# A mixture-of-experts kernel's end: the loop for surplus tokens moved behind the last up products, and the last down weights, down products and final norm done by column halves

## The chip, the cores and the metric

The kernel runs on one core of a Trainium2 chip. The metric is the device time of one execution in microseconds (us); lower is better. Engines are named as in the profile: PE is TensorE (PEld its weight loads), DVE is VectorE, ACT is ScalarE, POOL is GpSimd, and SP is the engine whose queue issues nearly all DMAs here. A letter q behind a name (SPq, PEq) means the engine's sequencer.

## The reference, cut to what matters

One layer over 256 tokens of width 1024: a norm, a projection, an mLSTM half and a differential-attention half, an output projection, then a hierarchical mixture of 32 experts and a last norm. Only the end of it is touched by the change:

```
    t = h.reshape(-1, d)                       # h = rmsnorm(x, norm2_g)
    ...                                        # router: 2 experts of one group per token, gates
    for e in range(N_EXPERTS):                 # 32 experts, width 512
        hid = jax.nn.silu(t @ w_eg[e]) * (t @ w_eu[e])
        out = out + gates[:, e:e + 1] * (hid @ w_ed[e])
    x = x + out
    return rmsnorm(x, normf_g)
```

Each of `w_eg`, `w_eu` and `w_ed` is 2 MB per expert in float32, so the expert weights alone are 192 MB.

## The kernel before

The kernel computes each expert only on the tokens that chose it. 128 slots (partitions) are shared by a group of two experts with 64 slots each or of four experts with 32 slots each; the last group has four. For each group PE gathers its tokens, transposed, with a one-hot matrix (`prep`), multiplies them by the gate and up weights (`gate`, `up`, L885), takes silu times up times the gate value, transposes that (`hidden`, L820 on DVE, L824 on PE, L827 on ACT), multiplies by the down weights (`down`, L902), splits the result into a high and a low part (ACT, then DVE) and scatters both back by a one-hot matrix into four PSUM accumulators `acc[j][t]`, where j is the half of the 1024 output columns and t the half of the 256 tokens. With four experts of 32 slots, a matmul uses 32 of PE's columns, and four matmuls of four experts run side by side; such a set of four is called a quad here.

Weights come in tiles of 1 MB: one expert, one half `hf` of the rows of a weight matrix (for `w_ed`: hf 0 holds the row blocks k = 0 and 1, hf 1 holds k = 2 and 3, each 1024 columns wide). SP issues these DMAs in the order gate, up, down of each group (`load`, `load_w`). Eight counters ("lanes") count landed DMAs in turn; each issue waits until the DMA eight places before it has landed, so that at most eight are open. In the last group (`LAST`), the tiles of hf 1 of `w_ed` come in three pieces: k = 2 whole (512 KB), then the two column halves of k = 3 (256 KB each).

An expert can have more tokens than slots. The surplus is done by a loop whose count `n_ov` is worked out on the chip (L1018 to L1077). Every engine reads `n_ov`, and branches. Where it is 0, an engine jumps to a block that adds to the counters what its own part of the loop would have added; SP's block also waits for the lanes that the loop's DMAs would use. So the loop stands in all engines' instruction streams even when no pass runs, and in the profiled execution none runs.

In the program, the loop stands right behind the last gate product. Behind the loop come the last `up` (`pu_l`, L1080), `hidden` into the tile `hT_l` (L1083), the final norm's gains spread over the partitions (`nfb`, L1087 on PE and L1088 on ACT), the last down products (L1094), their split (L1100, L1101), the scatter (L1105), and the final norm: `square` (L1109, sums of squares on ACT), `gain` (L1113, times `nfb` on DVE), `rms` (L1116 and L161 to L167) and `scale` with the output DMA (L1122 to L1127). `keep_warm` (L186) issues matmuls whose result nobody reads; their numbers between the last down products are `NW5`. Within an engine, instructions run in the order of the built program; a scheduler may move rows within a block, but none over the loop.

Of the kernel before, what the change touches and what calls it, by code (L numbers as in the profile page):

```python
# [10 lines left out]
F32 = mybir.dt.float32  # L11
# [5 lines left out]
OP = mybir.AluOpType  # L17
AX = mybir.AxisListType

P = 128  # L20
S = 256
NT = 2
D = 1024
KD = 8
H = 4
NE = 32
# [3 lines left out]
FF = 512  # L30
# [7 lines left out]
NWA, NWB, NWZ = 6, 11, 6  # L38
NPJ = 4
NST = 4  # L40
NWARM, NW1, NW2, NW3, NW5 = 9, 2, 10, 4, (0, 8, 4, 0)
NL = 3


# [1 line left out]
R_CW, R_CB, R_MN, R_MS, R_DA, R_N1, R_N2, R_NF = 0, 16, 20, 24, 28, 29, 37, 45  # L46
# [58 lines left out]
def kernel(ctx: ExitStack, tc: tile.TileContext,  # L105
                       x, w_in, w_out, w_eg, w_eu, w_ed, pack_a, pack_b, pack_m, out, dbg=None):
    nc = tc.nc
    V, A, G, T, SY = nc.vector, nc.scalar, nc.gpsimd, nc.tensor, nc.sync
    PS = bass.MemoryType.PSUM

    def dap(t, off, ap):
        return bass.AP(tensor=t.tensor, offset=t.offset + off, ap=ap)
# [26 lines left out]
    ident = ca[:, A_ID:A_ID + P]  # L139
# [3 lines left out]
    def col(i):  # L143
        return ca[:, A_COL + i:A_COL + i + 1]
# [10 lines left out]
    behind = [None, None]  # L155
# [25 lines left out]
    def keep_warm(n, pw, after=None):  # L181

        wide = warm[:, None, :].to_broadcast([P, 4, P])
        for _ in range(n):
            if after is None:
                T.matmul(pw, warm, wide, start=True, stop=True)  # L186
            else:
                with tc.issue_after(after.ins):
                    after = T.matmul(pw, warm, wide, start=True, stop=True)
# [92 lines left out]
    o = proj_T(0)  # L282
# [44 lines left out]
    o = proj_tok(512)  # L327
# [67 lines left out]
    o = proj_T(1536)  # L395
# [3 lines left out]
    o = proj_T(2048)  # L399
# [15 lines left out]
    o = proj_tok(2560)  # L415
    wo = []
    for j in range(2):
        for kk in (1, 0):
            w = w_half()
# [18 lines left out]
    for h in range(H):  # L438
# [115 lines left out]
    o = proj_T(1024, {2: po_ends[0], 4: po_ends[1], 5: po_ends[2], 6: po_ends[3]})  # L554
# [17 lines left out]
    acc = [[pacc.tile([P, 512], F32, name=f"acc{j}{t}") for t in range(NT)] for j in range(2)]  # L572
# [28 lines left out]
    for b, (c0, nc_) in enumerate(cols):  # L601
        j, cj = c0 // 512, c0 % 512
# [12 lines left out]
        for i in range(c0 // 256, (c0 + nc_) // 256):  # L615
# [16 lines left out]
            for m in range(2):  # L632
# [3 lines left out]
                for t in range(NT):  # L636
                    c = (m - first) * S + t * P
# [38 lines left out]
    def top8(name, v):  # L676
# [4 lines left out]
        for t in range(NT):  # L681
# [9 lines left out]
                    op=OP.not_equal)  # L691
# [47 lines left out]
    def pmm():  # L739
        return psm.tile([P, 512], F32, name="pmm", tag="pmm", bufs=4)  # L740
# [5 lines left out]
    order = [wa] + wbs[:7] + [wa] + wbs[7:9] + [wa] + wbs[9:] + [wa] + wzs[:2] + [wa] * 2 + wzs[2:]  # L746
    count, loaded = [0], [None]
# [6 lines left out]
    LAST = len(groups) - 1  # L754
    assert sum(map(len, groups)) == NE and len(groups[LAST]) == 4

    def load_w(src, rows, hf, pieces):

        w = []
        for _ in rows:  # L760
            w.append(order[count[0] % len(order)].tile([P, 4, 512], F32, name="w", tag="w"))
            count[0] += 1
        w = [v.rearrange("p a b -> p (a b)") for v in w]
        at = (0, *pieces)
        for c0, c1 in zip(at, pieces):
            for i, v in enumerate(w):
                o = hf * 2048 + c0
                if isinstance(rows[i], int):
                    r = dap(src, rows[i] * D * FF + o, [[4096, P], [1, c1 - c0]])
                else:  # L770
                    if isinstance(rows[i], bass.AP):
                        rows[i] = SY.value_load(rows[i], min_val=0, max_val=NE - 1)
                    r = of_expert(src, rows[i])[:, o:o + c1 - c0]
                with tc.issue_after(loaded[0].ins) if len(pieces) > 1 else nullcontext():
                    loaded[0] = SY.dma_start(v[:, c0:c1], r)
        return w

    def of_expert(src, e):

        return src.rearrange("o e d f -> (o e) (d f)")[bass.ds(e, 1)].rearrange("e (p n) -> (e p) n", p=P)  # L780
# [31 lines left out]
    def free(i):  # L812

        w = order[(count[0] + i) % len(order)].tile([P, 4, 512], F32, name="w", tag="w")
        return w.rearrange("p a b -> p (a b)")

    def hidden(n, sg_, pu_, gs, to=None):
        hid = mp.tile([P, 512], F32R, name="oH", tag="oH", bufs=1).bitcast(F32).rearrange("p (k s) -> p k s", k=4)

        V.scalar_tensor_tensor(hid[:n], sg_[:n].rearrange("p (q k) -> p k q", k=4), gs[:n, :1],  # L820
                               pu_[:n].rearrange("p (q k) -> p k q", k=4), op0=OP.mult, op1=OP.mult)
        pt = pmm()
        for k in range(4):
            T.transpose(pt[:, k * P:k * P + n], hid[:n, k], ident[:n, :n])  # L824
        hT = mp.tile([P, 512], F32R, name="oL", tag="oL", bufs=1).bitcast(F32) if to is None else to
        hT = hT.rearrange("p (k s) -> p k s", k=4)
        A.copy(hT[:, :, :n], pt.rearrange("p (k s) -> p k s", k=4)[:, :, :n])  # L827
        return hT
# [33 lines left out]
    def load(g):  # L862
        ws = {}
        src = {"g": w_eg, "u": w_eu, "d": w_ed}
        js = groups[g]
        rows = list(js) if js[0] < N_FIX else [permi[0:1, j:j + 1] for j in js]
        for n_, hf in [(n_, hf) for hf in range(2) for n_ in "gu"] + [("d", 0), ("d", 1)] if g == 0 else \
                [(n_, hf) for n_ in "gud" for hf in range(2)]:

            at = (1024, 1536, 2048) if g == LAST and (n_, hf) == ("d", 1) else (2048,)  # L870
            for i, w in enumerate(load_w(src[n_], rows, hf, at)):
                ws[n_, i, hf] = w
        return ws

    up_end = [None]

    def up(ws, n_, xg, p_=None, ks=range(KD)):
        if p_ is None:
            p_ = pgu()
        n = len(ws) // 6  # L880
        cap = P // n
        for k in ks:
            for i in range(n):
                k4 = k % 4
                up_end[0] = T.matmul(p_[i * cap:(i + 1) * cap], xg[:, k, i * cap:(i + 1) * cap],  # L885
                         ws[n_, i, k // 4][:, k4 * FF:(k4 + 1) * FF], start=(k == 0), stop=(k == KD - 1))
        return p_
# [4 lines left out]
        A.activation(sg_, up(ws, "g", xg) if p_ is None else p_, AF.Silu, scale=rs[:, :1])  # L892
        return sg_

    def down(ws, hT, ojs, ks=range(4)):
        n = len(ws) // 6
        cap = P // n
        for k in ks:
            for j in range(2):
                for i in range(n):  # L900
                    c0 = (k % 2) * D + j * 512
                    T.matmul(ojs[j][i * cap:(i + 1) * cap], hT[:, k, i * cap:(i + 1) * cap],  # L902
                             ws["d", i, k // 2][:, c0:c0 + 512], start=(k == 0), stop=(k == 3))
        return ojs

# [73 lines left out]
    ws = load(0)  # L979
# [20 lines left out]
    for pr in range(LAST):  # L1000
# [4 lines left out]
        hT = hidden(P, sg_, pu_, gs)  # L1005
# [7 lines left out]
    room = free(0)  # L1013
    sg_l = gate(ws, xg_l, rs_l, room[:, :FF])
    wx_free = [free(i) for i in range(1, 7)]
    tc.keep_in_program_order(A.preload_act_table_set(SET_EXP_LN))

    n_ov = nc.values_load(nov[0:1, 0:1], min_val=0, max_val=2 * S // (CAP // 2 + 1))  # L1018
# [58 lines left out]
                scatter(CAP, S_, oj, j)  # L1077


    pu_l = up(ws, "u", xg_l)  # L1080

    nfb, zt, jk, hT_l = (free(i) for i in range(7, 11))
    hT_l = hidden(P, sg_l, pu_l, gs_l, hT_l[:, :512])  # L1083
    for j in range(2):
        p_ = pmm()
        for k in range(4):
            T.matmul(p_[:, k * P:(k + 1) * P], col(R_NF + 4 * j + k).to_broadcast([P, P]), ident, start=True, stop=True)  # L1087
        A.copy(nfb[:, j * 512:(j + 1) * 512], p_)  # L1088
    ss = mp.tile([P, NT, 2], F32, name="ss")
    zt = [zt[:, t * D:(t + 1) * D] for t in range(NT)]  # L1090
    oj = [pgu(), pgu()]
    warm_to = pgu()
    for k, n in enumerate(NW5):
        down(ws, hT_l, oj, (k,))  # L1094
        if n:
            keep_warm(n, warm_to)
    oH = [jk[:, j * 512:(j + 1) * 512].bitcast(F32R) for j in range(2)]
    oL = [jk[:, (2 + j) * 512:(3 + j) * 512].bitcast(F32R) for j in range(2)]
    for j in range(2):
        A.copy(oH[j], oj[j])  # L1100
        V.tensor_tensor(oL[j], oj[j], oH[j].bitcast(F32), op=OP.subtract)  # L1101
    for o_ in (oH, oL):
        for j in range(2):
            for t in range(NT):
                T.matmul(acc[j][t], S_l[:, t * P:(t + 1) * P], o_[j], start=False, stop=(o_ is oL), skip_group_check=True)  # L1105

    def square(j, t):
        sq = mp.tile([P, KD, P], F32, name="xg", tag="xg", bufs=1).rearrange("p k s -> p (k s)")[:, :FF]
        A.activation(sq, acc[j][t], AF.Square, accum_out=ss[:, t, j:j + 1])  # L1109

    def gain(j, t):
        js = slice(j * 512, (j + 1) * 512)
        V.tensor_tensor(zt[t][:, js], acc[j][t], nfb[:, js], op=OP.mult)  # L1113
# [12 lines left out]
            V.tensor_scalar(z, z, rf, None, op0=OP.mult)  # L1126
        (A if E is A else SY).dma_start(dap(out, t * P * D + i * 512, [[D, P], [1, 512]]), z)  # L1127

    square(0, 0)
    gain(0, 0)  # L1130
    gain(0, 1)
    square(1, 0)
    rf = rms(0)
    square(0, 1)
    with tc.issue_after(behind[1].ins):
        gain(1, 0)
    with tc.issue_after(behind[0].ins):
        square(1, 1)
    scale(0, 0, V, rf)
    scale(0, 1, V, rf)  # L1140
    rf = rms(1)
# [30 lines left out]
```

## Time and profile before

| | |
|---|---|
| median of 3 runs | 613.75 us (613.34 to 614.83) |
| the profiled execution's own time | 614.0 us |
| its span, first to last instruction | 612.2 us |
| mean granted PE clock | 0.953 of full |
| PE busy | 537.4 us (88%) |
| DVE, ACT, POOL busy | 163.5, 124.5, 8.9 us |
| read from HBM | 221.39 MB, 365 GB/s over the span |

Outside the span lie 614.0 - 612.2 = 1.8 us. The page's table of 40 slices shows DMA at nine tenths or more from slice 15 to slice 38 at about 420 GB/s, and 37 and 69 GB/s in the last two slices. Its PE row reads 9 in nearly all of the middle, and 3, 8 and 3 in the last three slices. Most of the span is thus a stream of weights; the change touches what stands at the end of that stream.

### The profile page before, as it was taken

The page shows a single profiled execution, that of the slowest core. Times are in us where ns is not written, and L with a number is a line of the kernel's source. Part 1 is how long each engine was busy: PE and PEld are TensorE (multiplying, and loading weights), DVE is VectorE, ACT ScalarE, POOL GpSimd, SP SyncE. Part 2 cuts the span into 40 slices and gives each one's busy share as a digit, 9 for nine tenths or more (in the row PEclk, how much of TensorE's full clock was granted, in tenths as well). Part 3 has the DMA queues.
Part 4 walks back from the last instruction along what each step waited for, and adds up shares of the span by engine and source line. Part 5 has one row for each costly group of instructions (what it writes and reads, how often), then busy time and mean ns, then how long its engine had stood idle before and what let it go on. Part 6 is the DMA issues. An engine that isn't in the chain of part 4 may idle for free. (4 is left out here: it accounts for less than half of the span.)

```text
span 612.2 us, 8083 instructions
## 1 busy us (share of the span) xinstructions
PE 537.4 (88%) x3047; PEld 271.5 (44%) x3047; DVE 163.5 (27%) x472; ACT 124.5 (20%) x291; POOL 8.9 (1%) x19
## 2 busy tenths in 40 slices
PE   7999999998999999999799788799787799786383
PEld 5898779794543424344325223225223225221120
DVE  4774788745230202020200100100100100100004
ACT  4775477662100000010000000000100000010013
POOL 0000004001000000000000000000000000000000
PEclk8999999999999999999899799899989899798877
DMA  8965798968999999999999999999999999999911
GB/s 297 390 185 118 241 401 347 391 247 331 337 373 425 386 421 420 420 420 418 420 419 420 419 420 419 422 419 418 420 421 419 419 420 418 421 419 419 396 37 69
DMA packets 40764, 223.77 MB, mean 366 GB/s; under 512 B 3732, under 2 KB 6164, under 8 KB 16532
## 3 DMA queue, kind: packets, MB, share of 16 engines
q1 hardware_dynamic: 40436, 222.89, 91.0%
q8 instruction: 25, 0.41, 0.3%
q10 hardware_dynamic: 288, 0.35, 0.3%
q14 instruction: 15, 0.12, 0.0%
HBM read 221.39 MB, written 1.84 MB: 365 GB/s over the span
## 5 line engine op out<-in xcount | busy, mean ns | idle before, releaser
L885 PE MATMUL pmm<-w,xg 128*32 128x512 f32 (+1 forms) x1024 | 203.5, 624 | 18.3 <-DMA w<-in_w_eu_dram 13.5
L885 PEld LDWEIGHTS pmm<-w,xg 128*32 128x32 f32 (+1 forms) x1024 | 52.0, 123 | 140.1 <-issue 97.4
L902 PE MATMUL pmm<-w,oL 128*32 128x512 f32 (+1 forms) x448 | 97.6, 653 | 10.4 <-ACT oL L827 6.1
L902 PEld LDWEIGHTS pmm<-w,oL 128*32 128x32 f32 (+1 forms) x448 | 29.6, 131 | 70.9 <-issue 46.2
L233 DVE TENSOR_TENSOR wl<-w,wh 128x512 fp32r<-128x512 f32 (+1 forms) x72 | 44.6, 630 | 24.3 <-ACT wh L232 22.2
L834 DVE TENSOR_TENSOR oL<-pmm,oH 128x512 fp32r<-128x512 f32 x20 | 13.8, 691 | 133.5 <-PE pmm L902 104.3
L232 ACT ACTIVATE wh<-w 128x512 fp32r<-128x512 f32 (+1 forms) x72 | 41.0, 581 | 29.8 <-PE pj L263 13.1
L807 PEld LDWEIGHTS pmm<-Gm,x1c 128*128 128x128 f32 x352 | 40.6, 192 | 14.3 <-PE pmm L885 7.4
L807 PE MATMUL pmm<-Gm,x1c 128*128 128x128 f32 x352 | 43.8, 280 | 0.6 <-DVE ctr L977 0.6
L263 PE MATMUL pj<-hL,wh 128*128 128x256 f32 x128 | 36.3, 289 | 0.0
L833 ACT CAST oH<-pmm 128x512 fp32r<-128x512 f32 x20 | 11.7, 585 | 120.4 <-PE pmm L902 95.2
L261 PE MATMUL pj<-hH,wh 128*128 128x256 f32 x128 | 35.8, 291 | 0.0
L264 PE MATMUL pj<-hH,wl 128*128 128x256 f32 x128 | 35.7, 290 | 0.0
L808 DVE TENSOR_TENSOR xg<-pmm,cb 128x512 f32<-128x512 f32 (+1 forms) x24 | 14.9, 644 | 75.5 <-PE pmm L885 63.7
L827 ACT COPY oL<-pmm 128x512 f32<-128x512 f32 x10 | 5.8, 585 | 137.5 <-PE pmm L824 137.5
L892 ACT ACTIVATE oL<-pmm,rg 128x512 f32<-128x512 f32 x10 | 6.9, 687 | 89.3 <-PE pmm L885 64.9
L263 PEld LDWEIGHTS pj<-hL,wh 128*128 128x128 f32 x128 | 24.6, 192 | 0.1
L264 PEld LDWEIGHTS pj<-hH,wl 128*128 128x128 f32 x128 | 24.1, 192 | 1.4 <-issue 1.2
L261 PEld LDWEIGHTS pj<-hH,wh 128*128 128x128 f32 x128 | 24.3, 193 | 0.2
L902 PE MATMUL pmm<-w 128*32 128x512 f32 x64 | 11.9, 684 | 11.1 <-ACT w L827 11.1
L824 PE MATMUL pmm<-ca,oH 128*128 128x128 f32 x44 | 7.1, 283 | 16.2 <-DVE oH L820 16.2
L820 DVE SCALAR_TENSOR_TENSOR oH<-oL,rg,pmm 128x512 f32<-128x512 f32 x10 | 11.2, 1119 | 25.8 <-PE pmm L885 22.7
(344 smaller groups left out, 481.9 us busy)
## 6 DMA issues: line engine op xcount, KB each, us to landing
w<-in_w_eg_dram SPq DMA_DIRECT2D x64, 1024.0 KB, 19.8
w<-in_w_eu_dram SPq DMA_DIRECT2D x64, 1024.0 KB, 19.8
w<-in_w_ed_dram SPq DMA_DIRECT2D x60, 1024.0 KB, 19.8
w<-in_w_in_dram SPq DMA_DIRECT2D x10, 1024.0 KB, 14.4
w<-in_w_out_dram SPq DMA_DIRECT2D x4, 1024.0 KB, 12.8
w<-in_w_ed_dram SPq DMA_DIRECT2D x4, 512.0 KB, 17.8
w<-in_w_ed_dram SPq DMA_DIRECT2D x8, 256.0 KB, 7.8
w<-in_w_in_dram SPq DMA_DIRECT2D x3, 512.0 KB, 8.7
```

The costliest lines, as they stand in the source:

```text
L232: A.activation(wh, raw, AF.Copy)
L233: V.tensor_tensor(wl, raw, wh.bitcast(F32), op=OP.subtract)
L261: T.matmul(om, wh[:, cs], hH[:, k], start=(k == 0 and m % 2 == 0), stop=False, skip_group_check=True)
L263: T.matmul(om, wh[:, cs], hL[:, k], start=False, stop=False, skip_group_check=True)
L264: T.matmul(om, wl[:, cs], hH[:, k], start=False, stop=(k == KD - 1), skip_group_check=True)
L807: T.matmul(px_[:, i * P:i * P + n], x1c[:, t, k0 + i], G_[:, t], start=(t == 0), stop=(t == NT - 1))
L808: V.tensor_tensor(xg[:, k0:k0 + per, :n], px_.rearrange("p (k s) -> p k s", k=4)[:, :per, :n], cb[:, B_N2 + k0:B_N2 + k0 + per, None].to_b ...
L820: V.scalar_tensor_tensor(hid[:n], sg_[:n].rearrange("p (q k) -> p k q", k=4), gs[:n, :1], pu_[:n].rearrange("p (q k) -> p k q", k=4), op0= ...
L833: A.copy(oH[:n], oj[:n])
L834: V.tensor_tensor(oL[:n], oj[:n], oH[:n].bitcast(F32), op=OP.subtract)
L885: up_end[0] = T.matmul(p_[i * cap:(i + 1) * cap], xg[:, k, i * cap:(i + 1) * cap], ws[n_, i, k // 4][:, k4 * FF:(k4 + 1) * FF], start=(k = ...
L902: T.matmul(ojs[j][i * cap:(i + 1) * cap], hT[:, k, i * cap:(i + 1) * cap], ws["d", i, k // 2][:, c0:c0 + 512], start=(k == 0), stop=(k == 3))
```

## The change

1. The last `up`, `hidden` and the two `nfb` products and copies stand ahead of the loop; ACT's table load, the reading of `n_ov`, and the loop follow them.
2. `load_w` loses its pieces. The last group's down weights are loaded by `load_by_columns`: first the left 512 columns of hf 0 and of hf 1 of all four experts (512 KB each), then the right 512 columns of hf 0 (512 KB each), of k = 2 and of k = 3 (256 KB each). That is 20 DMAs in place of 16, in runs of 2 KB per partition (512 float32 numbers).
3. The last down products, split and scatter are done for the left columns (j = 0) first and then for the right columns (`last_down`). The squares and gains of the left columns follow the left scatter; at the end ACT makes the two squares of the right columns one after the other.
4. `NW5` goes from (0, 8, 4, 0) to (8, 4, 4, 3): 8 warm matmuls between the two row halves of the left columns, 4 behind the left scatter, 4 behind k = 0 and 1 of the right columns, 3 behind k = 2.

```diff
-NWARM, NW1, NW2, NW3, NW5 = 9, 2, 10, 4, (0, 8, 4, 0)
+NWARM, NW1, NW2, NW3, NW5 = 9, 2, 10, 4, (8, 4, 4, 3)
...
+    def load_by_columns(src, rows):
+
+        w = [[slot() for _ in rows] for _ in range(2)]
+        for hf, k0, k1, j in ((0, 0, 2, 0), (1, 0, 2, 0), (0, 0, 2, 1), (1, 0, 1, 1), (1, 1, 2, 1)):
+            for v, e in zip(w[hf], rows):
+                at = [a.rearrange("p (k c) -> p k c", k=2)[:, k0:k1, j * 512:(j + 1) * 512]
+                      for a in (v, of_expert(src, e)[:, hf * 2048:(hf + 1) * 2048])]
+                with tc.issue_after(loaded[0].ins):
+                    loaded[0] = SY.dma_start(*at)
...
-            at = (1024, 1536, 2048) if g == LAST and (n_, hf) == ("d", 1) else (2048,)
-            for i, w in enumerate(load_w(src[n_], rows, hf, at)):
-                ws[n_, i, hf] = w
+            if g < LAST or n_ != "d":
+                for i, w in enumerate(load_w(src[n_], rows, hf)):
+                    ws[n_, i, hf] = w
+        if g == LAST:
+            for hf, w_ in enumerate(load_by_columns(w_ed, rows)):
+                for i, w in enumerate(w_):
+                    ws["d", i, hf] = w
...
     wx_free = [free(i) for i in range(1, 7)]
+    pu_l = up(ws, "u", xg_l)
+
+    nfb, zt, jk, hT_l = (free(i) for i in range(7, 11))
+    hT_l = hidden(P, sg_l, pu_l, gs_l, hT_l[:, :512])
+    for j in range(2):
+        p_ = pmm()
+        for k in range(4):
+            T.matmul(p_[:, k * P:(k + 1) * P], col(R_NF + 4 * j + k).to_broadcast([P, P]), ident, start=True, stop=True)
+        A.copy(nfb[:, j * 512:(j + 1) * 512], p_)
     tc.keep_in_program_order(A.preload_act_table_set(SET_EXP_LN))
 
     n_ov = nc.values_load(nov[0:1, 0:1], min_val=0, max_val=2 * S // (CAP // 2 + 1))
...
-    pu_l = up(ws, "u", xg_l)
...
-    for k, n in enumerate(NW5):
-        down(ws, hT_l, oj, (k,))
-        if n:
-            keep_warm(n, warm_to)
...
+    def last_down(j, pieces):
+        end = None
+        for ks, n in pieces:
+            with tc.issue_after((end or last_end[0]).ins):
+                down(ws, hT_l, oj, ks, (j,))
+                end = down_end[0]
+            if n:
+                keep_warm(n, warm_to, end)
+        A.copy(oH[j], oj[j])
+        V.tensor_tensor(oL[j], oj[j], oH[j].bitcast(F32), op=OP.subtract)
+        for o_ in (oH, oL):
+            for t in range(NT):
+                last_end[0] = T.matmul(acc[j][t], S_l[:, t * P:(t + 1) * P], o_[j], start=False, stop=(o_ is oL),
+                                       skip_group_check=True)
+
+    last_down(0, (((0, 1), NW5[0]), ((2, 3), 0)))
+    for t in range(NT):
+        square(0, t)
+        gain(0, t)
+    keep_warm(NW5[1], warm_to, last_end[0])
+    last_down(1, (((0, 1), NW5[2]), ((2,), NW5[3]), ((3,), 0)))
     square(1, 0)
     rf = rms(0)
-    square(0, 1)
...
-    with tc.issue_after(behind[0].ins):
-        square(1, 1)
+    square(1, 1)
```

Up to the end of the last gate product, every engine has the same instructions in the same order; SP's loads differ from the last group's down weights on. Two engines show the move.

ACT, around the loop, before. L892 is the silu of the last gate product (L827 and L833 above it belong to the group before); L827 behind the loop is the copy into `hT_l` (a tile w), L1088 the two copies into `nfb`:

```order
L827 COPY oL<-pmm 128x512
L833 CAST oH<-pmm 128x512 x2
L892 ACTIVATE w<-pmm,rg 128x512
L1016 ACT_TABLE_LOAD
L1018 TENSOR_LOAD nov
L1019 COMPARE_AND_BRANCH
```

and behind the loop:

```order
L1019 UNCONDITIONAL_BRANCH
L827 COPY w<-pmm 128x512
L1088 COPY w<-pmm 128x512 x2
L1100 CAST w<-pmm 128x512
L1109 ACTIVATE xg,ss<-acc_1395 128x512
L1100 CAST w<-pmm 128x512
L1109 ACTIVATE xg,ss<-acc_1397 128x512
L1109 ACTIVATE xg,ss<-acc_1396 128x512
L162 ACTIVATE rsr<-rsv 128x1
L163 ACTIVATE rsr<-rsr 128x1
L1109 ACTIVATE xg,ss<-acc_1398 128x512
```

The same places of ACT in the changed kernel (acc_1395 and acc_1396 are the accumulators of the left columns, acc_1397 and acc_1398 those of the right):

```order
L904 ACTIVATE w<-pmm,rg 128x512
L836 COPY w<-pmm 128x512
L1036 COPY w<-pmm 128x512 x2
L1037 ACT_TABLE_LOAD
L1039 TENSOR_LOAD nov
L1040 COMPARE_AND_BRANCH
```

and behind the loop:

```order
L1040 UNCONDITIONAL_BRANCH
L1140 CAST w<-pmm 128x512
L1110 ACTIVATE xg,ss<-acc_1395 128x512
L1110 ACTIVATE xg,ss<-acc_1396 128x512
L1140 CAST w<-pmm 128x512
L1110 ACTIVATE xg,ss<-acc_1397 128x512
L1110 ACTIVATE xg,ss<-acc_1398 128x512
L162 ACTIVATE rsr<-rsv 128x1
L163 ACTIVATE rsr<-rsr 128x1
```

Three copies went from behind the loop to ahead of it, and the two squares of the left columns ahead of the second cast.

PE, behind the loop, before: the last up products (L885), the four transposes of `hidden`, the `nfb` products, the first six down products and the first warm matmul:

```order
L1019 UNCONDITIONAL_BRANCH
L885 MATMUL pmm<-w,xg 32x512 x32
L824 MATMUL pmm<-ca,oH 128x128 x4
L1087 MATMUL pmm<-ca 128x128 x8
L902 MATMUL pmm<-w 32x512 x6
L186 LDWEIGHTS warm
L186 MATMUL pmm<-warm 128x512
```

and PE's end, before (23 down products in a row behind the warm matmuls, and the scatter of the left columns into acc_1395 and acc_1396 among the last ones):

```order
L902 MATMUL pmm<-w 32x512 x23
L1105 MATMUL acc_1395<-w,S__3781 128x512
L1105 MATMUL acc_1396<-w,S__3781 128x512
L902 MATMUL pmm<-w 32x512
L1105 MATMUL acc_1395<-w,S__3781 128x512
L1105 MATMUL acc_1396<-w,S__3781 128x512
L902 MATMUL pmm<-w 32x512 x2
```

PE ahead of the loop in the changed kernel (L897 are the last gate and up products, L833 the transposes, L1035 the `nfb` products):

```order
L897 MATMUL pmm<-w,xg 32x512 x62
L833 MATMUL pmm<-ca,oH 128x128 x4
L1035 MATMUL pmm<-ca 128x128 x8
L1039 TENSOR_LOAD nov
L1040 COMPARE_AND_BRANCH
```

and PE's end in the changed kernel (the last of 3 warm matmuls, the last quad, and the scatter of the right columns):

```order
L189 LDWEIGHTS warm
L189 MATMUL pmm<-warm 128x512
L914 MATMUL pmm<-w 32x512 x4
L1144 MATMUL acc_1397<-w,S__3781 128x512
L1144 MATMUL acc_1398<-w,S__3781 128x512
L1144 MATMUL acc_1397<-w,S__3781 128x512
L1144 MATMUL acc_1398<-w,S__3781 128x512
```

On PE all up products now stand ahead of the loop, all 64 down products stay behind it, in order of columns, and only four of them stand between the last warm matmul and the last scatter.

## Rows read from the trace of the kernel before

**Rows 1.** Chain that ended last, from 540 us: start us, length us, what.
```profile
583.88 0.59 ACT w L827
...
584.52 3.65 PE pmm L902 x12
588.17 2.94 PE pmm L186 x12
591.12 6.14 PE pmm L902 x46
...
600.29 1.03 PE pmm L902 x4
...
601.35 0.59 ACT w L1100
...
601.99 1.24 PE acc L1105 x3
...
604.02 0.69 ACT xg L1109 x2
...
607.34 0.75 DVE w L1124
```

**Rows 2.** Timeline: start us, length us, engine, line, operation [idle before <-releaser].
```profile
546.94 33.20 SPq L775 DMA_DIRECT2D w<-in_w_ed_dram  x16
...
548.29 2.11 PE L885 MATMUL pmm<-w,xg 128*32 128x512 f32 x4 [0.30 <-PEq L1019]
548.74 1.28 ACT L1016 ACT_TABLE_LOAD   x1
...
571.00 0.66 PE L824 MATMUL pmm<-ca,oH 128*128 128x128 f32 x4 [1.26 <-DVE oH L820]
...
571.49 1.95 PE L1087 MATMUL pmm<-ca 128*128 128x128 f32 x16
583.88 0.58 ACT L827 COPY w<-pmm 128x512 f32<-128x512 f32 x1 [33.86 <-SPq L1019]
```

**Rows 3.** Line L1019, the loop's branch, on SP: count, ns min/median/max, first and last start.
```profile
L1019 SPq EVENT_SEMAPHORE  x7: 17/17/17, 580.4 to 583.9; - x7
```

**Rows 4.** Busy time by stretch; the last three columns are PE clock, DMA share, GB/s.
```profile
566.00:568.00 2.00, 2.00 (x16) 0.47 (x11) 0.00 (x0) 0.00 (x0) 0.00 (x0) 0.50 1.01 418
572.00:574.00 2.00, 1.44 (x13) 1.25 (x12) 0.00 (x0) 0.00 (x0) 0.00 (x0) 1.00 1.02 414
574.00:576.00 2.00, 0.00 (x0) 0.00 (x0) 0.00 (x0) 0.00 (x0) 0.00 (x0) 1.00 1.01 406
579.00:580.00 1.00, 0.00 (x0) 0.00 (x0) 0.00 (x0) 0.00 (x0) 0.00 (x0) 0.50 1.08 375
580.00:582.00 2.00, 0.00 (x0) 0.00 (x0) 0.00 (x0) 0.00 (x0) 0.00 (x0) 0.50 0.87 314
584.50:585.00 0.50, 0.48 (x3) 0.21 (x6) 0.00 (x0) 0.50 (x2) 0.00 (x0) 0.50 0.01 4
588.00:590.00 2.00, 2.00 (x11) 0.87 (x9) 0.00 (x0) 0.00 (x0) 0.00 (x0) 0.84 0.00 0
```

**Rows 5.** Line L775 from 530 us: the down loads' issues, and DMA times to landing.
```profile
L775 SPq DMA_DIRECT2D w<-in_w_ed_dram x16: 332/333/336, 546.9 to 579.8; - x16
...
DMA to landing us min/median/max: 5.9/19.0/20.2
```

**Rows 6.** Timeline of PE's weight loads: two quads apart at full, two at half clock.
```profile
540.32 0.13 PEld L885 LDWEIGHTS pmm<-w,xg 128*32 128x32 f32 x4 [0.30 <-issue]
540.75 0.13 PEld L885 LDWEIGHTS pmm<-w,xg 128*32 128x32 f32 x4 [0.30 <-issue]
...
564.41 0.16 PEld L885 LDWEIGHTS pmm<-w,xg 128*32 128x32 f32 x8 [2.35 <-DMA w<-in_w_eu_dram]
...
565.83 0.21 PEld L885 LDWEIGHTS pmm<-w,xg 128*32 128x32 f32 x4 [0.64 <-issue]
566.68 0.21 PEld L885 LDWEIGHTS pmm<-w,xg 128*32 128x32 f32 x4 [0.64 <-issue]
```

**Rows 7.** The down products on PE: count, ns min/median/max, first and last start.
```profile
L902 PE MATMUL pmm<-w x64: 592/592/1064, 584.5 to 600.7; 128*32 128x512 f32 x64
```

More of the change, by code (lines that the diff above doesn't have):

```diff
@@ L755, with slot, load_w @@
     assert sum(map(len, groups)) == NE and len(groups[LAST]) == 4
[L757 to L775, printed above, removed]
+    def slot():
+        w = order[count[0] % len(order)].tile([P, 4, 512], F32, name="w", tag="w")
+        count[0] += 1
+        return w.rearrange("p a b -> p (a b)")
+    def load_w(src, rows, hf):
+        w = [slot() for _ in rows]
+        for i, v in enumerate(w):
+            o = hf * 2048
+            if isinstance(rows[i], int):
+                r = dap(src, rows[i] * D * FF + o, [[4096, P], [1, 2048]])
+            else:
+                if isinstance(rows[i], bass.AP):
+                    rows[i] = SY.value_load(rows[i], min_val=0, max_val=NE - 1)
+                r = of_expert(src, rows[i])[:, o:o + 2048]
+            loaded[0] = SY.dma_start(v, r)
+        return w
+    def load_by_columns(src, rows):
[6 more added lines that the diff above has]
+                    loaded[0] = SY.dma_start(*at)
         return w
@@ L868, in load @@
                 [(n_, hf) for n_ in "gud" for hf in range(2)]:
-            at = (1024, 1536, 2048) if g == LAST and (n_, hf) == ("d", 1) else (2048,)
-            for i, w in enumerate(load_w(src[n_], rows, hf, at)):
-                ws[n_, i, hf] = w
+            if g < LAST or n_ != "d":
[5 more added lines that the diff above has]
+                    ws["d", i, hf] = w
         return ws
-    up_end = [None]
+    up_end, down_end = [None], [None]
     def up(ws, n_, xg, p_=None, ks=range(KD)):
@@ L893, in gate, with down @@
         return sg_
-    def down(ws, hT, ojs, ks=range(4)):
+    def down(ws, hT, ojs, ks=range(4), js=range(2)):
         n = len(ws) // 6
@@ L898, in down @@
         for k in ks:
-            for j in range(2):
+            for j in js:
                 for i in range(n):
                     c0 = (k % 2) * D + j * 512
-                    T.matmul(ojs[j][i * cap:(i + 1) * cap], hT[:, k, i * cap:(i + 1) * cap],
+                    down_end[0] = T.matmul(ojs[j][i * cap:(i + 1) * cap], hT[:, k, i * cap:(i + 1) * cap],
                              ws["d", i, k // 2][:, c0:c0 + 512], start=(k == 0), stop=(k == 3))
@@ L1077 @@
                 scatter(CAP, S_, oj, j)
-    pu_l = up(ws, "u", xg_l)
[L1082 to L1088, printed above, removed]
     ss = mp.tile([P, NT, 2], F32, name="ss")
@@ L1092 @@
     warm_to = pgu()
-    for k, n in enumerate(NW5):
-        down(ws, hT_l, oj, (k,))
-        if n:
-            keep_warm(n, warm_to)
     oH = [jk[:, j * 512:(j + 1) * 512].bitcast(F32R) for j in range(2)]
     oL = [jk[:, (2 + j) * 512:(3 + j) * 512].bitcast(F32R) for j in range(2)]
[L1099 to L1105, printed above, removed]
     def square(j, t):
@@ L1127, in scale @@
         (A if E is A else SY).dma_start(dap(out, t * P * D + i * 512, [[D, P], [1, 512]]), z)
-    square(0, 0)
-    gain(0, 0)
-    gain(0, 1)
+    last_end = [up_end[0]]
+    def last_down(j, pieces):
[18 more added lines that the diff above has]
+    last_down(1, (((0, 1), NW5[2]), ((2,), NW5[3]), ((3,), 0)))
     square(1, 0)
     rf = rms(0)
-    square(0, 1)
     with tc.issue_after(behind[1].ins):
         gain(1, 0)
-    with tc.issue_after(behind[0].ins):
-        square(1, 1)
+    square(1, 1)
     scale(0, 0, V, rf)
```

## The prediction

> **What bounds the kernel now.** I read the chain that ended last first. Its last 28 us hold nothing but the end of the program: ACT's copy into `hT_l` at 583.88, then PE's down products and warm matmuls without a pause to 597.3, the split, the scatter and the norm [rows 1]. So from 583.88 on the time is set by PE and by what starts it. Second, the timeline around that start. The transposes whose result ACT copies were done at 571.00 + 0.66 = 571.7, and the `nfb` products at 571.49 + 1.95 = 573.4, but the copy began at 583.88; the 33.86 us of idle time before it are put down to SP at L1019, the branch of the loop [rows 2]. SP could not come there sooner: its down loads are issued one by one until 579.8, paced by landings [rows 5], and in the skipped loop it works through seven waits and additions to the counters from 580.4 to 583.9 [rows 3]. ACT's copy waits for one of those additions. Third, the DMA rates by stretch: 418 GB/s while the loads come in runs of 8 KB, 406 in the stretch of runs of 4 KB, 375 when only pieces in runs of 2 KB are left, then 314 as the queue drains, and the last bytes come at 584.5 to 585 [rows 4]; I take 584.6. So PE starts 64 down products when all their weights have already landed: 601.32 - 584.6 = 16.7 us of PE work and waiting [rows 1] lie behind the stream of weights, then 612.2 - 601.32 = 10.9 us of tail.
>
> **The change part by part.**
>
> *The loop.* ACT's copy now stands ahead of the branch, so nothing of SP's is between it and the transposes: it ends at 571.7 + 0.59 = 572.3 [rows 1, 2]. The two `nfb` copies follow at 0.59 each, the second behind its product, to 574.0, then the table load of 1.28 [rows 2] to 575.3. What is queued behind the branch now: on PE every down product, on ACT the casts. PE's own crossing showed a gap of 0.30 us between matmuls [rows 2]; ACT and DVE cross while they have nothing to do. From both sides: 0.30, and at most the 3.5 us that SP took for its seven steps [rows 3], if the crossing were slow for PE too. I take 0.30, the row of the same engine; PE is through at 573.75. SP crosses last, behind its loads, and only the output DMAs, 5 us later than the last product, stand behind it.
>
> *The loads.* Of the 8.39 MB of down weights, 4.19 came in runs of 8 KB, 2.10 of 4 KB and 2.10 of 2 KB; now all come in runs of 2 KB. By the rates of [rows 4]: 4190/375 - 4190/418 = 1.15 us and 2097/375 - 2097/406 = 0.43 us, together 1.6 us, on the path. Bounds: nothing (the number of bytes is the same), and 4.8 us if these 6.29 MB came at the 314 GB/s of the draining queue (3.3 and 1.5 by the same two parts). I take 1.6, since the row with 375 is the one in which the queue was full of this very kind of piece. The last landing moves from 584.6 to 586.2 (584.6 to 589.4). Four more issues at 0.33 us [rows 5] hide behind SP's waits for landings. Left columns of hf 0 are there at about 570.0, of hf 1 at 575.6, right columns of hf 0 at 581.2 (2.10 MB at 375 GB/s = 5.6 us each, from the last up weights at 564.41 [rows 6]), and k = 2 half-way from there to the last, at about 583.7.
>
> The Trainium skill (DMA: Bandwidth & Descriptors, Bandwidth, Measured) speaks against this: it wants DMAs batched to 1 MiB or more and gives a fixed 2.0 us per DMA beside bytes at 436 GB/s, so twenty of 256 to 512 KB one after the other would be an estimated 20 x 2.0 + 8.39 MB/436 GB/s = 59 us. The rows show eight open at once and 375 GB/s with 256 KB pieces alone; that price would be rival C.
>
> *PE behind the branch.* Prices: a quad takes 0.43 us at full and 0.85 at half clock, from weight load to weight load [rows 6]; a warm matmul 2.94/12 = 0.25 [rows 1]; cast, subtraction and scatter 603.23 - 601.35 = 1.9, and some 0.2 more for the last matmul [rows 1]. Left columns: two quads from 573.75 (their weights are there), 0.9; 8 warm, 2.0; to 576.6, past the landing at 575.6; two quads, 0.9, to 577.5, when ACT has been free since 575.3; split and scatter to 579.6; 4 warm to 580.6. Right columns: wait for 581.2, two quads to 582.1, 4 warm to 583.1, wait for 583.7, a quad to 584.2, 3 warm to 584.9, wait for 586.2. So PE is ahead of the stream by 1.3 us at the end, and of the 64 products only the last quad is behind it: 0.59 us for a matmul from its start to its end [rows 7]. The last product ends at 586.8. The 19 warm matmuls and the left half's split, scatter, squares and gains cost nothing because they lie under loads; without that cover they would cost 19 x 0.25 + 1.9 us.
>
> *The clock.* These prices are at full clock. PE's clock was full at 572 to 574, still full at 574 to 576 with PE idle, and half at 579 [rows 4]; it came back 4.1 us after work began at 584.52, since the stretch 588 to 590 reads 0.84, full from about 588.6. Now PE begins at 573.75, before the fall, and has no wait over 1.3 us from there on. I take full clock to the end.
>
> *The tail.* Before, ACT made a square of the right columns (L1109), one of the left, Ln and Exp, then the last square. Now both left squares are done early and two right squares come first. The first token half's norm still waits for one right square only, and ACT still makes one more before its Ln; I count 0.0, with 0.7 us (one square, by the 0.69 at 604.02 in [rows 1]) as the most that it can give or take. So 10.9 us stay.
>
> *Sum.* Span: 586.2 + 0.6 + 10.9 = 597.7 against 612.2, a gain of 14.5 us. From the profiled execution's own 614.0 that gives 599.5; the median of the runs, 613.75, is 0.25 lower, so 599.2. Its own range: with no price for the loads and the square gained, 596.9; with the last landing at 589.4, 602.4.
>
> **The rivals.**
>
> A: PE, not the stream, ends last, because the clock falls. For it: PE is idle for 1.26 us ahead of the transposes at 571.00 [rows 2], and the clock was at half at 566 to 568 [rows 4]. Against it: it was full in the same place in this trace from 572 on. With every PE price from 573.75 doubled: two quads 1.7, 8 warm 4.0, two quads 1.7, split and scatter 3.0, 4 warm 2.0, two quads 1.7, 4 warm 2.0, a quad 0.85, 3 warm 1.5, the last 1.0: 19.5 us, to 593.2, and about 1.1 more in the last scatter: span 605.2, time 606.7. With half of that stretch at half clock PE ends about 588.8, and the time is about 602.
>
> B: the change does not free PE: something behind the branch still waits for SP. Then PE starts at about 586.3, at half clock for 4.1 us; the work of 0.9 + 2.0 + 0.9 + 2.1 + 1.0 + 0.9 + 1.0 + 0.4 + 0.8 + 0.6 = 10.6 us becomes 12.6, ends at 598.9, and the time is 611.4. For it: SP was the releaser before. Against it: the down products before waited for ACT's copy, which has moved.
>
> C, slower: the small loads starve. If each piece held its lane as long as the median of 19.0 us [rows 5], whatever its size, the 20 pieces would need two and a half rounds: the lane that issued a piece at 554 would issue the next at 573 and the last at 592, landing at 611, and the time would be 611 + 0.6 + 10.9 + 1.6 = 624. It is slower than now once the last landing is after 601.32 - 0.6 = 600.7. Against it: in [rows 5] the shortest landing is 5.9 us, among the last pieces of 256 KB, with the queue at 375 GB/s: landing time follows the bytes ahead in the queue.
>
> **How the numbers follow.** Forecast 0.78, A 0.11, B 0.08, C 0.03. The predicted time is the forecast's, 599.2. Its own range holds some nine tenths of its 0.78; up to 604.5 come the nearer half of A and a loss of some 2 us that I have not seen, so 597.0 to 604.5 holds about 0.8. About 0.3% (1.8 us) is what a measurement of this kernel can tell from no change. B lies 2.4 us below now, so a third of it may come within that: faster 0.94, same 0.03, slower 0.03.
>
> **What would show it.** In the profile after: ACT's copy into `hT_l` at about 571.7 with the transposes as releaser, and no wait for the branch on ACT over a few us; the first down product near 573.8; the last bytes of weights near 586.2 at about 375 GB/s through the down loads; the last down product released by a DMA, not by PE's own queue, and ended within 1 us of that landing; PE's clock full from 574 to the scatter; 10.9 us from there to the end. A PE that runs without waits up to the last product means A; a first down product after 583 means B; a rate under 300 GB/s with fewer bytes open means C.

## The result and the profile after

The changed kernel takes 598.52 us (median of 4 runs, 597.43 to 599.4) against 614.29 us for the kernel before beside it (4 runs): a ratio of 0.9743, 95% interval 0.9717 to 0.9769. The forecast was 599.2 us, in a range of 597.0 to 604.5. The profiled execution took 597.43 us with a span of 595.6 us, at a mean granted clock of 0.971 (before: 612.2 and 0.953).

The timeline of after, in the columns of [rows 2], around the place where ACT's copy stood idle:

```profile
562.68 3.62 PE L897 MATMUL pmm<-w,xg 128*32 128x512 f32 x26 [1.48 <-DMA w<-in_w_eu_dram]
...
568.26 0.58 ACT L836 COPY w<-pmm 128x512 f32<-128x512 f32 x1 [21.24 <-PE pmm L833]
...
570.41 1.92 PE L914 MATMUL pmm<-w 128*32 128x512 f32 x16 [0.40 <-PEq L1040]
570.65 1.28 ACT L1037 ACT_TABLE_LOAD   x1
...
584.17 0.14 PEld L914 LDWEIGHTS pmm<-w 128*32 128x32 f32 x2 [0.46 <-DMA w<-in_w_ed_dram]
585.26 0.58 ACT L1140 CAST w<-pmm 128x512 fp32r<-128x512 f32 x1 [5.86 <-PE pmm L914]
```

The copy into `hT_l` is released by the transposes (PE L833) and no longer by SP, 15.6 us earlier than in [rows 2]. The first down product follows at 570.41, with 0.40 us for the branch, where it stood at 584.52. SP still works through its seven steps, 1 us earlier than in [rows 3], and in this trace nobody waits for them:

```profile
L1040 SPq EVENT_SEMAPHORE  x7: 17/17/17, 579.4 to 582.8; - x7
```

The chain that ended last, in the columns of [rows 1]:

```profile
570.41 1.92 PE pmm L914 x16
572.33 1.83 PE pmm L189 x8
574.17 1.90 PE pmm L914 x16
...
579.07 1.85 PE pmm L914 x16
...
583.64 1.59 PE pmm L914 x8
...
585.26 0.59 ACT w L1140
...
591.07 0.75 DVE w L1125
```

The last product ends at 583.64 + 1.59 = 585.2 (before 601.3), so the tail to the end of the span is 10.4 us (before 10.9). The stretches, in the columns of [rows 4]:

```profile
562.00:564.00 2.00, 1.32 (x14) 0.42 (x18) 0.00 (x0) 0.00 (x0) 0.00 (x0) 1.00 1.04 386
574.00:576.00 2.00, 2.00 (x17) 0.42 (x16) 0.00 (x0) 0.00 (x0) 0.00 (x0) 1.00 1.05 388
580.00:582.00 2.00, 2.00 (x20) 0.48 (x14) 0.12 (x1) 0.00 (x0) 0.00 (x0) 1.00 0.77 267
583.50:584.00 0.50, 0.50 (x4) 0.15 (x6) 0.00 (x0) 0.00 (x0) 0.00 (x0) 1.00 0.02 8
588.00:590.00 2.00, 0.00 (x0) 0.00 (x0) 1.86 (x10) 1.33 (x6) 0.00 (x0) 0.61 0.00 0
```

The clock is full until the scatter is over (1.00 in every stretch up to 588.0). The stream of weights runs at 380 to 388 GB/s in the stretches of 2 us from 562 to 578, and ends in the stretch before 584.0. Line L784 answers to [rows 5]: 20 issues, and landings far from starved.

```profile
L784 SPq DMA_DIRECT2D w<-in_w_ed_dram x20: 332/386/3169, 545.2 to 578.9; - x20
...
DMA to landing us min/median/max: 5.3/10.8/18.8
```

### The profile page after: what moved, and what is told of

Its sections match the earlier page's. It is cut to its first block, busy times and chain, and to the rows that moved or that the text cites. A ratio compares the mean times of both kernels' runs of the same rounds, so it can differ in the third digit from the quotient of the medians.

```text
span 595.6 us, 8111 instructions
## 1 busy us (share of the span) xinstructions
PE 529.3 (89%) x3054; PEld 268.4 (45%) x3054; DVE 163.2 (27%) x472; ACT 124.7 (21%) x291; POOL 9.7 (2%) x19
## 5 line engine op out<-in xcount | busy, mean ns | idle before, releaser
L897 PE MATMUL pmm<-w,xg 128*32 128x512 f32 (+1 forms) x1024 | 198.8, 615 | 21.8 <-DMA w<-in_w_eu_dram 15.7
L897 PEld LDWEIGHTS pmm<-w,xg 128*32 128x32 f32 (+1 forms) x1024 | 50.9, 122 | 139.6 <-issue 95.1
L833 PE MATMUL pmm<-ca,oH 128*128 128x128 f32 x44 | 7.2, 289 | 16.2 <-DVE oH L829 16.2
L833 PEld LDWEIGHTS pmm<-ca,oH 128*128 128x128 f32 x44 | 5.0, 150 | 22.3 <-issue 20.1
```

## The experiments

Three theories were on trial. Theory 1 is the prediction's: ACT's copy waited for SP's skip of the loop, and the gain is that wait. Theory 2: the gain is the columns, whose left half is worked off under the loads. Theory 3: PE's chain, not the stream of weights, sets the new end. Theory 4 came up on the way: both end level.

This table holds the readings that all runs share, us. "Up" is the start of the last set of up products, released by the last up landing; "bytes" is the end of the weights' stream, read in stretches of 0.2 us; "product" is the end of the last down product. All readings but the ratio are from one profiled execution of each kernel. Runs measured together stand together, and each ratio is to the kernel before measured beside them; the first row is the profile of before, the second the first one of after.

| kernel | ratio to before (95%) | up | bytes | product | span |
|---|---|---|---|---|---|
| before | | 564.4 | 584.6 | 601.3 | 612.2 |
| after | 0.9743 (0.9717 to 0.9769) | 562.7 | 583.8 | 585.2 | 595.6 |
| c0, after again | 0.9751 (0.9726 to 0.9776) | 561.8 | 582.8 | 585.9 | 596.3 |
| e1, loop only | 0.9786 (0.9753 to 0.9819) | 562.6 | 582.6 | 585.5 | 596.4 |
| e2, columns only | 0.9991 (0.9973 to 1.0009) | 561.9 | 583.2 | 598.7 | 609.1 |
| e7, tile swap | 0.9809 (0.9765 to 0.9852) | 563.7 | 584.2 | 587.5 | 598.4 |
| e3, no warm | 0.9752 (0.9724 to 0.9779) | 562.5 | 583.6 | 585.2 | 595.7 |
| e4, warm doubled | 0.9811 (0.9787 to 0.9835) | 562.0 | 583.4 | 589.8 | 600.3 |
| e5, rows first | 0.9819 (0.9798 to 0.9839) | 562.9 | 583.2 | 588.8 | 599.5 |
| e6, no loop | 0.9762 (0.9733 to 0.9792) | 564.1 | 585.4 | 587.4 | 597.8 |
| c1, after again | 0.9762 (0.9734 to 0.9790) | 563.7 | 585.4 | 587.0 | 597.4 |
| e8, norm weights first | 0.9769 (0.9737 to 0.9800) | 562.4 | 584.4 | 585.9 | 596.4 |
| e9, and half the warm | 0.9749 (0.9720 to 0.9778) | 562.3 | 583.8 | 585.3 | 595.7 |
| e10, e1 with less warm | 0.9771 (0.9743 to 0.9799) | 563.4 | 583.8 | 586.9 | 597.8 |

**The two halves of the change apart.** First the control, then the kernel before with the loop alone moved:

> The changed kernel, unaltered, beside the kernel before on this chip. Every theory: 597.4 to 599.5 us, and a last up landing and last down landing that show how far two executions of one program lie apart upstream (562.7 and 583.7 us in the first profile of it, 564.4 and 584.6 in that of the kernel before).

```diff
+    pu_l = up(ws, "u", xg_l)
+    nfb, zt, jk, hT_l = (free(i) for i in range(7, 11))
+    hT_l = hidden(P, sg_l, pu_l, gs_l, hT_l[:, :512])
+    for j in range(2):
...
+        A.copy(nfb[:, j * 512:(j + 1) * 512], p_)
     tc.keep_in_program_order(A.preload_act_table_set(SET_EXP_LN))
...
-    pu_l = up(ws, "u", xg_l)
...
-        A.copy(nfb[:, j * 512:(j + 1) * 512], p_)
```

> The kernel before with the loop alone put behind the up products, ScalarE's copies and the norm's weights; loads, order of the down products and norm are those of before. Theory 1 (the gain is ScalarE's copy of the hidden values, which no longer waits for SyncE's skip of the loop): the copy ends near 572 instead of 583.9, the products run as their weights land, and the time is 597.5 to 601 us. Theory 2 (the gain is the columns: the left half's norm lies under the loads): this kernel has no columns, so it keeps most of the time of before, 606 to 610 us.

598.96 us beside 597.76 for the control and 612.27 for before. Then the columns alone, the changed kernel with the loop back ahead of the up products:

```diff
-    pu_l = up(ws, "u", xg_l)
...
     with tc.If(n_ov > 0):
...
+    pu_l = up(ws, "u", xg_l)
```

> The changed kernel with the loop back ahead of the up products: the columns, their loads and their norm alone. Theory 1: ScalarE's copy ends near 583.5, behind SyncE's skip of the loop; TensorE then needs the 14.8 us that it took in the changed kernel for the products and what lies between them (570.41 to 585.24), some of it at the half clock, so 608 to 615 us. Theory 2: the columns carry the gain, 600 to 604 us.

612.49 us: while ACT waits for SP, the columns are worth nothing that can be measured. (This kernel also carries the change's 19 warming matmuls where before has 12.) Timeline of e1, then of e2:

```profile
568.22 0.59 ACT L827 COPY w<-pmm 128x512 f32<-128x512 f32 x1 [21.17 <-PE pmm L824]
...
570.37 1.92 PE L902 MATMUL pmm<-w 128*32 128x512 f32 x12 [0.40 <-PEq L1028]
```

```profile
582.45 0.59 ACT L836 COPY w<-pmm 128x512 f32<-128x512 f32 x1 [34.83 <-SPq L1031]
...
583.09 3.23 PE L914 MATMUL pmm<-w 128*32 128x512 f32 x16 [12.18 <-ACT w L836]
```

In e1 PE releases the copy, in e2 SP does, and from there e2 needs 15.6 us to its last product, almost all of it behind the stream. Theory 2 falls, theory 1 stands.

**Why the copy waited.** A wait for SP does not by itself say that the loop's place is at fault. In the built program of before, ACT's copy waits for a count that SP adds on behalf of the loop's own loads, because the tile that `hT_l` got lies in the same memory as a tile that one of those loads writes: the landings of the down loads bring that lane's counter to 464, SP adds the last 16, and the copy waits for 480. So one line of before was changed:

```diff
-    nfb, zt, jk, hT_l = (free(i) for i in range(7, 11))
+    hT_l, nfb, jk, zt = (free(i) for i in range(7, 11))
```

> The kernel before with one line changed: the hidden values go into the tile that the norm's weights had, and these into the tile of the hidden values. The loop stays where it was. In the built program of before ScalarE's copy into the hidden values waits for a count that SyncE adds for the loop's own loads, since that tile is one of those that the loop loads into; the tile that it gets here has no such wait. Theory 1 in this narrower form (the wait belongs to the tile, not to the place of the loop): the copy ends near 572 and the time is 597.5 to 602 us. Rival (an engine that stands behind the loop's branch waits for the loop whatever tile it writes): 612 to 615 us, as before.

600.35 us: 11.9 of the 14.5 us between before and the control, with the loop where it was. The wait belongs to the tile, and moving the loop is one way to be rid of it. Timeline of e7:

```profile
569.73 0.59 ACT L827 COPY w<-pmm 128x512 f32<-128x512 f32 x1 [20.38 <-PE pmm L824]
...
583.48 0.59 ACT L1100 CAST w<-pmm 128x512 fp32r<-128x512 f32 x1 [11.38 <-SPq L1019]
```

The second row shows a second wait of the same kind: the first cast, into the tile `jk`, is still released by SP. It costs little: against e1 the last product is 2.0 us later, and the stream ended 1.6 us later.

**What sets the new end.** Warming matmuls are work on PE that nothing waits for by itself, so they were taken out and doubled:

```diff
-NWARM, NW1, NW2, NW3, NW5 = 9, 2, 10, 4, (8, 4, 4, 3)
+NWARM, NW1, NW2, NW3, NW5 = 9, 2, 10, 4, (0, 0, 0, 0)
```

> The changed kernel without the 19 warming matmuls that stand between its down products; they add nothing to the output. In its two profiles they take 4.5 to 4.7 us of TensorE's time from 570 to 585. Theory 3 (TensorE's own chain, not the stream, sets the end): the last product moves forward until it meets the last landing plus one quad of 1.0 us, so by 0.5 us (last bytes 583.7, last product's end 585.2 in the first profile) to some 2 us (582.6 and 585.8 in the second), a time of 596 to 597.5 us where the changed kernel has 598. Theory 1 as it was forecast (the stream sets the end, TensorE is 1.3 us ahead of it): no gain, 597.5 to 598.5. Rival on the clock: without them the granted clock falls to one half before the end, the last quad, the scatter's two pairs and the waits behind them take 2 to 3 us longer, 599 to 601 us.

> The changed kernel with twice the warming matmuls, 38 for 19: 4.5 us more on TensorE between 570 and 585, nothing else. Theory 3 (TensorE's chain sets the end): nearly all of it shows, 601.5 to 603 us. Theory 1 as it was forecast (1.3 us of slack ahead of the stream, as quads were priced at half of what they take): 3 us or less, 599.5 to 601.2 us. If the stream set the end by far, no change, 598.

(In the second, (16, 8, 8, 6).) Without them: 598.51 us, no gain, and the clock stayed full to the scatter. Doubled: 602.25 us, by the ratios 3.0 to 4.2 us more than after in its three comparisons (0.9811 against 0.9762 to 0.9743, of 614), for 4.1 us of added work: from the first down product to the end of the last one PE took 18.4 us, and 14.3 in c0, where it hardly waited. PE has at most about a microsecond of slack, yet it can't end earlier. The waits of after and of c0 for down weights (which line waited for what: us, times, longest):

```profile
PEld pmm L914 <- DMA w<-in_w_ed_dram: 0.9, 2, 0.5
```

```profile
PEld pmm L914 <- DMA w<-in_w_ed_dram: 0.4, 1, 0.4
```

Those of e3, and its last two products on the timeline:

```profile
PEld pmm L914 <- DMA w<-in_w_ed_dram: 3.5, 4, 1.2
...
PEld pmm L914 <- SPq L1040: 2.5, 5, 0.5
```

```profile
583.52 0.14 PEld L914 LDWEIGHTS pmm<-w 128*32 128x32 f32 x2 [0.53 <-DMA w<-in_w_ed_dram]
584.18 0.14 PEld L914 LDWEIGHTS pmm<-w 128*32 128x32 f32 x2 [0.52 <-DMA w<-in_w_ed_dram]
```

The time that the warming took became waits for weights. The five waits put down to SP's skip are such waits too: in the built program PE's down products wait only for counts that the landings alone reach, and SP adds to these counts when the same landings have come. PE now meets the last pieces one by one, 0.66 us apart, about what 256 KB take at 385 GB/s (0.68); its last product starts at 584.18, in after at 584.17. So the two ends lie level: theory 4.

Next, half of the stream's price taken back: the first half of the rows in runs of 8 KB, both column halves together.

```diff
-        for hf, k0, k1, j in ((0, 0, 2, 0), (1, 0, 2, 0), (0, 0, 2, 1), (1, 0, 1, 1), (1, 1, 2, 1)):
+        for hf, k0, k1, j in ((0, 0, 2, None), (1, 0, 2, 0), (1, 0, 1, 1), (1, 1, 2, 1)):
```

> The changed kernel with the first half of the down weights (rows 0 to 1023 of each partition's run, both column halves together) loaded in 8 KB runs as before, and only the second half by columns. The order of the products is kept. If the 2 KB runs cost 0.8 us of stream (the two profiles' 21.0 against 20.2 us from the last up landing to the last bytes), half of it comes back, the rate is near 418 GB/s in the first half, and the last bytes come 0.4 us earlier. Theory 1 (stream): 597.3 to 598. Theory 3 (TensorE's chain): the left half's last weights come at another time and TensorE does not start earlier, so no gain, 597.8 to 599.

602.69 us: every theory missed. The stream did shorten, from 21.1 to 20.3 us (up to bytes), but the time grew by about 4 us (0.9819 against 0.9743 to 0.9762). Timeline of e5:

```profile
572.90 1.90 PE L915 MATMUL pmm<-w 128*32 128x512 f32 x10 [1.21 <-DMA w<-in_w_ed_dram]
...
578.23 1.90 PE L915 MATMUL pmm<-w 128*32 128x512 f32 x10 [0.27 <-DMA w<-in_w_ed_dram]
...
580.17 0.59 ACT L1141 CAST w<-pmm 128x512 fp32r<-128x512 f32 x1 [8.03 <-PE pmm L915]
...
588.87 0.59 ACT L1141 CAST w<-pmm 128x512 fp32r<-128x512 f32 x1 [5.38 <-PE pmm L915]
```

The right columns of hf 0 now land ahead of the left columns of hf 1, PE takes its products in order, and the left half's first cast comes at 580.17 instead of 576.09. The 8.7 us of PE's work from that cast to the second one then run past the stream's end at 583.2. Here the weights have to land in the order in which PE takes them.

The loop itself was left out, to see what it still costs in its new place:

```diff
-    n_ov = nc.values_load(nov[0:1, 0:1], min_val=0, max_val=2 * S // (CAP // 2 + 1))
-    with tc.If(n_ov > 0):
-        with tc.For_i(0, n_ov, 1):
...
```

> The changed kernel without the loop for surplus tokens (left out wholly; it runs no turn on this input, so what is left out is the test, the skip of each engine and the instructions that stand in its body). Theory 1: the loop now costs TensorE the 0.30 us at its branch and nothing else on the path, SyncE's skip (579.4 to 582.8 us) lies beside work that no engine waits for: 597 to 598.3 us. Rival (the skip still delays what stands behind it, through ScalarE's table load, the branch on five engines and the counts that SyncE adds): over 2 us faster, 594 to 596.

599.34 us, not to be told from after (0.9762, interval 0.9733 to 0.9792): the skip costs nothing on the path that these runs can tell. The Trainium skill (Runtime: NRT & Kernel Launch, Instruction fetch mechanics) says that a taken branch to a target outside the prefetched pages stalls its engine on a fetch; PE's gap at this branch is 0.40 us in after, and without the branch nothing is gained; no run here shows such a stall on the path.

**Looking for something better.** The products that lay out `nfb` were put ahead of the last up products (e8), and then the warming was cut as well, to (4, 2, 2, 2) (e9):

```diff
-    pu_l = up(ws, "u", xg_l)
     nfb, zt, jk, hT_l = (free(i) for i in range(7, 11))
-    hT_l = hidden(P, sg_l, pu_l, gs_l, hT_l[:, :512])
     for j in range(2):
...
         A.copy(nfb[:, j * 512:(j + 1) * 512], p_)
+    pu_l = up(ws, "u", xg_l)
+    hT_l = hidden(P, sg_l, pu_l, gs_l, hT_l[:, :512])
```

> The changed kernel, unaltered, as the control for the two that follow: 597.4 to 599.5 us by every theory.

> The changed kernel with the eight products that lay out the norm's weights, and their two copies, ahead of the last up products, so that TensorE crosses the loop's branch 1.5 us earlier (the down products start near 568.9 instead of 570.4 where the last up landing is at 562.7). Theory 3 (TensorE's chain alone sets the end): 1.5 us faster than the changed kernel, 596.3 to 597. Theory 4, after the runs without and with double warming (TensorE and the stream end level: no gain from less on TensorE, 4 us lost from 4.5 us more): 0 to 0.6 us faster, 597.3 to 598.4, the 1.5 us turning into waits for the last down weights. Rival: the products now stand in the way of the last up products or of the scatter of the group before, and the time is up to 2 us longer.

> The kernel of the run above with 10 warming matmuls for 19 (2.1 us less of TensorE's time): TensorE is then some 3.6 us ahead of where it was. Theory 3: 3 us faster than the changed kernel or more, near 595. Theory 4: as the run above, within 0.5 us of it, since the last landing and the products behind it (1.7 us from the last bytes to the last product's end in two profiles) hold.

598.96 and 597.89 us beside 599.24 for the control: neither can be told from it. PE started its down products 6.3 us behind "up" (568.77 and 568.55) instead of 7.7 (571.40 in c1), and ended 1.5 us behind the last bytes all the same, as theory 4 has it. In e8 part of the lead went to the clock, which was half for most of the stretch 568 to 572, as the first row shows; the second is e9, which has the same code up to its first warming matmul at 570.4:

```profile
568.00:572.00 4.00, 3.23 (x16) 0.68 (x16) 0.00 (x0) 1.87 (x2) 0.00 (x0) 0.59 1.06 385
```

```profile
568.00:572.00 4.00, 3.45 (x24) 0.95 (x24) 0.00 (x0) 1.72 (x2) 0.00 (x0) 1.00 1.06 385
```

Last, whether the columns can be spared altogether (e1 with (0, 4, 0, 0) in place of (0, 8, 4, 0)):

> The kernel before with the loop alone moved, as in the run of that name, and 4 warming matmuls for 12. In that run the last product ended 2.9 us behind the last bytes of weights (585.5 and 582.6 us) with TensorE never waiting, and 12 warming matmuls took 2.7 us. Theory 4 (end = the later of TensorE's chain and some 1.5 us behind the last bytes): the last product comes 1.5 to 1.8 us earlier, near 584, and the time is about 1.5 us under that run's, level with the changed kernel, 597 to 598.5 us, without any loads by columns. Rival (the columns carry the last microsecond or two, by the left half's norm that lies under the loads): it stays at that run's 599 us or above.

599.82 us: theory 4's number missed. The last product came 3.1 us behind the last bytes, as in e1 (2.9) and e7 (3.3), however little PE had to do before: with products by rows, PE takes the left columns' scatter (L1105) between the products of the right columns' last quad, and most of this stands behind the last bytes (583.8). Timeline of e10:

```profile
583.48 0.73 PE L1105 MATMUL acc<-w,S__3781 128*128 128x512 f32 x2
...
584.15 1.05 PE L902 MATMUL pmm<-w 128*32 128x512 f32 x2
...
585.12 0.73 PE L1105 MATMUL acc<-w,S__3781 128*128 128x512 f32 x2
...
585.79 1.05 PE L902 MATMUL pmm<-w 128*32 128x512 f32 x4
```

By columns that distance is 1.4 to 1.7 us in the five profiles where PE met the stream (after, c1, e3, e8, e9), and the tail is 10.4 against 10.9 us. So the columns give 1.5 + 0.5 us and take about 1 us of stream. That leaves about 1 us, as between e1 and its control (1.2 us). The intervals overlap, so this is a sum of profile readings, not a measured gain. No kernel tried beat the changed one beyond the uncertainty.

## Why the prediction was right, and which of its steps were not

**What bounded the kernel, and the loop: right.** e1, e2 and e7 show that ACT's copy and its wait for SP held nearly all of the 14.5 us between before and the control: 13.3 come back with the loop alone moved, 11.9 with the tile alone changed, and none with the wait left in. The copy's releaser became the transposes and PE's crossing cost 0.40 us (forecast 0.30). The copy came 3.4 us earlier than forecast, and so did the first down product (570.41 for 573.8). Of this 1.7 us is the stream, which reached the last up landing sooner in that execution (562.68 against 564.42), and 1.7 us the last up products, at full clock there (3.62 us) and at half in before (5.32 us). No run puts either down to the change: "up" lies from 561.8 to 564.1 us in the ten profiles with loads wholly or half by columns and from 562.6 to 564.4 in the four with the loads of before, and with either loads the last up products ran at full clock in some profiles (after, e1) and at half in others (c0, before).

**The loads: mis-sized.** The term was 1.6 us. From "up" to "bytes" the stream takes 20.0 to 20.5 us with the loads of before (before, e1, e7, e10) and 21.0 to 22.0 with those of the change (after, c0, c1, e2, e3, e4, e6, e8, e9), so the price is about 1 us, inside the bounds of 0 to 4.8. The 375 GB/s taken from [rows 4] came from one microsecond near the queue's end; a full queue of loads in runs of 2 KB moved 380 to 388. The prediction's two workings do not meet either: at 375 GB/s, 8.39 MB from 564.41 on would end at 586.8, and its sum has 586.2.

**PE's prices: wrong by a factor of two.** The step "a quad takes 0.43 us from weight load to weight load" failed. The built program has 32 down products (on PE behind the loop in before 6 + 23 + 1 + 2), and the profile has 64 rows for them in [rows 7]: each float32 product leaves two rows for the matmul and two for the weight load. So the "64 down products", in the section on the change as in the prediction, are 32, and a set of four weight loads in [rows 6] is half a quad. A quad takes 1.92/2 = 0.96 us (eight products in the 16 rows at 570.41). With that price the "1.3 us ahead of the stream" shrinks to waits of 0.9 us in all in after, and to none at the end in c0, where the last product ended 3.1 us behind the last bytes. The doubled warming shows the same. That the time still came out within 0.7 us is partly luck: PE began 3.4 us earlier than forecast in that execution. As an estimate, with the 14.3 us of c0 from the forecast start at 573.75 the last product would have ended at 588.1 and not 586.8, and with the measured tail the time would have been about 600.0 us, still inside the range.

**Behind the last landing: 0.6 us forecast, 1.4 measured,** from the last bytes to the last product's end; the wait there ended at 584.17, and a product is 1.07 us from its start to its end. The 0.59 us of [rows 7] was one row, so about half of a product.

**The tail: 10.9 forecast, 10.4 measured,** within the 0.7 that was allowed. The clock was full to the scatter, as forecast.

**The sum.** Span: forecast 597.7, measured 595.6. Last bytes 583.8 for 586.2 (-2.4, of which 1.7 came from upstream), the last product 0.8 later behind them, the tail 0.5 shorter: -2.1. Over the runs the median was 598.52 for a forecast of 599.2; other profiles of the same kernel had spans of 596.3 and 597.4.

**The rivals.** A (PE ends last because the clock falls) did not happen as told: the clock held. But PE does set the end in c0, at full clock; the trace bore out the outcome that was to mean A, without A's cause, and its price is at most about 2 us and not 3 to 7. B is refuted for the changed kernel, and e7's cast shows that it was a fair rival: a second tile had the same wait. C is refuted by landings of 5.3 to 18.8 us, median 10.8. The Trainium skill's price of 2.0 us for each DMA, weighed there, stands in DMA: Bandwidth & Descriptors, Anatomy of one DMA, as a fit for one DMA on GpSimd's path. It is not borne out for the loads here, which SP issues: with several pieces open at once the whole price of going to runs of 2 KB was about 1 us over 8.39 MB.

## What to carry to other kernels

When an engine idles for a semaphore of a loop that it has nothing to do with, look which tile the waiting instruction writes: another tile, which cost one line here, gave 11.9 of the 13.3 us that moving the loop alone gave. After such a wait is gone, count what stands behind the last landing and in which order the landings come: here the stream and the in-order engine then ended level, and work taken off the engine bought nothing. Before pricing instructions from rows of a trace, compare their number with the program's.

## What was not expected of the hardware

- A float32 product of 128x32 by 128x512 leaves two rows each for its matmul and its weight load (64 rows for 32 products).
- Four products of four experts that run as a quad take 0.96 us together; taken one at a time as their weights land, they stood 0.66 us apart (e3), with little lost, since the landings themselves were about 0.68 us apart.
- The same program reached its last up landing at 561.8, 562.7 and 563.7 us in three profiles, and its last 13 up products took 3.62 us at full clock in two of them and 5.73 at half clock in the third (c0).
